# Second norm: the shift added behind the transposes, by ScalarE and VectorE, instead of ahead of them by GpSimd

## The chip, the cores and the metric

One core of a Trainium2 chip runs the kernel. Its engines run side by side, each through its own list of instructions in order: TensorE (PE; PEld is its weight load), VectorE (DVE), ScalarE (ACT), GpSimd (POOL) and SyncE (SP, which issues DMAs). Engines wait for each other by semaphores. The metric is the device time of one execution in microseconds, median of several runs.

## What is computed

A transformer block over 512 tokens of width 1024: an adaptive norm, three attention branches, gates, an output projection, a second adaptive norm and a feed-forward layer. What matters here stands behind the output projection:

```python
x = x + gate1 * (merged @ w_o[l])

u2 = rmsnorm(x, norm_mlp[l]) * (1.0 + scale2) + shift2
h = jnp.square(jax.nn.relu(u2 @ w_ff1[l]))
x = x + gate2 * (h @ w_ff2[l])
```

`shift2` has 1024 values, one for each feature; `u2` is 512 tokens by 1024 features.

## The kernel before

All products are float32 accuracy out of three products of rounded parts: each operand is split into a high part (a rounded copy, written by ACT) and a low part (the operand less its high part, written by DVE or POOL). For `u2` these are the tiles `u2h` and `u2l`.

Tokens lie in four tiles of 128 (t = 0 to 3), features in two halves of 512 (g = 0, 1). The output projection (`token_major`, tiles `po`, weights `hi_wo`, `lo_wo`) makes tokens in rows: first the left half of the features for all tokens, then the right half, each in the order tokens 0, 1, then 2, 3. Behind each right half comes the second norm of that tile of tokens, in this chain:

- `put_x1`: DVE multiplies the product by the gate (`ot`, L1208), POOL adds x (L1209), ACT takes squares and the root (L1212, L1214).
- `norm2` (L1227): DVE inverts the root and makes `tn` = x times 1/rms times (1 + scale) for each half (L1232); POOL adds the shift `b2` (L1233). `b2` is a row of 1024 values that was copied to all 128 partitions by `bcast`; in the profile it is called `bc_b`.
- `turn2` (L1235): PE turns the half's four blocks of 128x128 into one PSUM bank (`u2p`), so that features lie on the partitions.
- `split2` (L1240): ACT copies the bank into `u2h`, DVE writes the bank less `u2h` into `u2l`.

I call the work of `split2` on one (t, g) a group; there are eight, in the order (0,0), (0,1), (1,0), (1,1), (2,0), (2,1), (3,0), (3,1). The PSUM banks for `u2p` rotate among three (tag "S").

Then the feed-forward layer begins in `ff1_halves`, with the first 512 of its columns taken in two halves of tokens (0, 1, then 2, 3), four outputs of 24 products each (L1290, `pf`). The first half stands while tokens 2, 3 are still being normed. The weights' own splits (`hi_f`, `lo_f`, L224 and L236) are put between the groups on the same engines.

The order on every engine is fixed by hand: `Flow` counts the products that PE is given, and a step put with `flow.at(n, ...)` is written to its engine's list when n more have been given:

```python
flow.at(14, lambda: norm2(t))
for g in range(2):
    flow.at((30, 28, 31, 29)[t] + 6 * g, lambda g=g: turn2(t, g))
    flow.at((33, 31, 34, 32)[t] + 6 * g, lambda g=g: split2(t, g))
```

Of the kernel before, what the change touches and what calls it, by code (L numbers as in the profile page):

```python
# [13 lines left out]
F32 = mybir.dt.float32  # L14
F32R = mybir.dt.float32r
AF = mybir.ActivationFunctionType
ALU = mybir.AluOpType
# [102 lines left out]
def block_kernel(ctx: ExitStack, tc: tile.TileContext, x, c, rel_bias, ada_w, ada_b, norm_mix, w_in,  # L120
                 gate_b, diff_lambda, diff_subln, dsa_kv_norm, dsa_w_uv, w_br_a, w_br_b, w_br_c, w_o,
                 norm_mlp, w_ff1, w_ff2, norm_final, onehot, out):
    nc = tc.nc
# [16 lines left out]
    def bank(tag, name):  # L140
        return ps.tile([128, 512], F32, tag=tag, name=name, bufs=banks[tag])

    def big_tile(name, dt=F32, shape=(128, 8, 512)):
        return big.tile(list(shape), dt, tag="big", name=name)
# [284 lines left out]
    for a, b, tag in ((0, 512, "S"), (512, 640, "T")):  # L429
        tps = bank(tag, f"tps{a}")  # L430
# [274 lines left out]
    bias = {}  # L705
# [220 lines left out]
    mod = dram.tile([4, 1024], F32, name="mod")  # L926
# [253 lines left out]
    mx = mixing.enter_context(tc.tile_pool(name="mx", bufs=1))  # L1180

    def bcast(pool, name, src):
        t = pool.tile([128, 1024], F32, name=f"bc_{name}")
        nc.gpsimd.dma_start(t, bass.AP(tensor=src.tensor, offset=src.offset, ap=[[0, 128], [1, 1024]]))
        return t
# [5 lines left out]
        nc.gpsimd.dma_start(x1[:, t], x[t * 128:(t + 1) * 128])  # L1191
    a2 = bcast(mx, "a2", mod[2:3])
    nmb = bcast(mx, "nm", norm_mlp)
    b2 = bcast(mx, "b2", mod[1:2])

    def hs(h):
        return slice(h * 512, (h + 1) * 512)

    sq = {t: s1(f"sq{t}", 2) for t in range(NT)}
    tns, tps = {}, {}  # L1200
    sq_early = s1("sq_early")
    u2h, u2l = big_tile("u2h", F32R), big_tile("u2l", F32R)

    def put_x1(h):
        def evac(t, p):
            xs, ss = x1[:, t, hs(h)], sq[t]
            tt = mx.tile([128, 512], F32, tag="t5", name=f"ot{h}{t}", bufs=3)
            nc.vector.tensor_tensor(tt, p, g1[:, hs(h)], op=ALU.mult)  # L1208
            nc.gpsimd.tensor_tensor(xs, xs, tt, op=ALU.add)  # L1209

            def square():
                nc.scalar.activation(tt, xs, AF.Square, accum_out=ss[:, h:h + 1])  # L1212
                if h == 1:
                    nc.scalar.activation(ss[:, 1:2], ss[:, 1:2], AF.Sqrt, bias=ss[:, 0:1], scale=1.0 / D)  # L1214

            flow.at(9, square)
            if h == 0:
                flow.at(14, lambda: nc.vector.tensor_scalar(ss[:, 0:1], ss[:, 0:1], 1.0 / D, EPS, op0=ALU.mult,
                                                            op1=ALU.add))
            else:  # L1220
# [4 lines that stand above are left out]
        return evac  # L1225

    def norm2(t):  # L1227
        r = sq[t][:, 1:2]
        nc.vector.reciprocal(r, r)
        for g in range(2):  # L1230
            tn = tns[t, g] = mx.tile([128, 512], F32, tag="tn", name=f"tn{t}{g}", bufs=4)
            nc.vector.scalar_tensor_tensor(tn, x1[:, t, hs(g)], r, a2[:, hs(g)], op0=ALU.mult, op1=ALU.mult)  # L1232
            nc.gpsimd.tensor_tensor(tn, tn, b2[:, hs(g)], op=ALU.add)  # L1233

    def turn2(t, g):  # L1235
        tp = tps[t, g] = bank("S", f"u2p{t}{g}")
# [1 line left out]
            nc.tensor.transpose(tp[:, k * 128:(k + 1) * 128], tns[t, g][:, k * 128:(k + 1) * 128], ident)  # L1238

    def split2(t, g):  # L1240
        tv = tps[t, g].rearrange("p (k q) -> p k q", k=4)
        dh = u2h[:, 4 * g:4 * g + 4, t * 128:(t + 1) * 128]
        nc.scalar.activation(dh, tv, AF.Copy)
        nc.vector.tensor_tensor(u2l[:, 4 * g:4 * g + 4, t * 128:(t + 1) * 128], tv, dh.bitcast(F32), op=ALU.subtract)

    flow.run(token_major(["wo00", "wo01"], mh, ml, ((0, 1), (2, 3)), put_x1(0), "po0", PAIR))
    nc.vector.scalar_tensor_tensor(a2, a2, 1.0, nmb, op0=ALU.add, op1=ALU.mult)
# [334 lines left out]
```

## Time and profile before

| | us |
|---|---|
| median of three runs | 843.79 |
| the three runs | 839.05, 843.79, 844.58 |
| the profiled execution, whole | 841.24 |
| its span, first to last instruction | 839.5 |

The profiled execution's own time is 1.74 us over its span. PE is busy for 96% of the span, so a time can be won or lost only where PE waits or is made to wait; the stretch that the change touches lies between 455 us (its loads) and 520 us (the second half of the first `ff1` columns).

### The profile page before, as it was taken

Reading aid. Unit: us, or ns where it says so; the run is one execution under the profiler, and the core shown is the slowest. Engines: PE = TensorE matmul, PEld = TensorE weight load, DVE = VectorE, ACT = ScalarE, POOL = GpSimd, SP = SyncE. Lnnn points to the kernel's source line nnn. Section 1 sums busy time; section 2 is a strip of 40 time slices with the busy share of each in tenths; the row PEclk is TensorE's granted clock in tenths of the full one; section 3 lists DMA queues with packets and bytes.
Section 4 is the critical chain, followed back from the end, with each engine's and each line's share of the span. In section 5 each row is a group of like instructions: output and inputs, shape, how many; then the busy total and the mean of one; then the engine's idle time right before and its main releaser. Section 6 shows DMA issues by size and latency. Waiting matters only on the chain. (4 is left out here: it accounts for less than half of the span.)

```text
span 839.5 us, 10498 instructions
## 1 busy us (share of the span) xinstructions
PE 808.7 (96%) x3865; PEld 644.8 (77%) x3865; DVE 570.8 (68%) x992; ACT 411.7 (49%) x712; POOL 186.9 (22%) x130
## 2 busy tenths in 40 slices
PE   5899999999999999899999989999999999999996
PEld 4778867678777776557787879888888888888885
DVE  5866785678878359885445685874678567857554
ACT  7655634552434365345652446554553356335433
POOL 2014322202562224552247370000000000010020
PEclk9999999999999999999999999999999999999998
DMA  9946451133656376512135528113511441172202
GB/s 308 347 136 207 172 195 66 51 100 110 196 194 215 95 264 189 164 35 92 50 101 197 206 68 322 60 51 114 188 50 51 162 140 50 51 248 102 99 4 100
DMA packets 81535, 116.48 MB, mean 139 GB/s; under 512 B 4590, under 2 KB 53274, under 8 KB 81484
## 3 DMA queue, kind: packets, MB, share of 16 engines
q1 hardware_dynamic: 78812, 107.73, 39.0%
q0 software_dynamic: 2672, 8.09, 2.7%
q8 instruction: 30, 0.49, 0.2%
q14 instruction: 21, 0.17, 0.1%
HBM read 110.25 MB, written 8.17 MB: 141 GB/s over the span
## 5 line engine op out<-in xcount | busy, mean ns | idle before, releaser
L1266 PE MATMUL pf<-u2h,hi_f 128*128 128x512 f32 x224 | 87.1, 389 | 0.0
L1268 PE MATMUL pf<-u2l,hi_f 128*128 128x512 f32 x224 | 87.1, 389 | 0.0
L1270 PE MATMUL pf<-u2h,lo_f 128*128 128x512 f32 x224 | 87.1, 389 | 0.0
L947 DVE SCALAR_TENSOR_TENSOR adacc<-adch,cond,adacc 128x512 f32<-128x512 f32 x56 | 61.5, 1098 | 3.9 <-DMA adch<-in_ada_w_dram 3.4
L236 DVE TENSOR_TENSOR lo_f<-raw_f,hi_f 128x1024 fp32r<-128x1024 f32 x38 | 46.6, 1255 | 16.9 <-ACT hi_f L224 16.9
L1436 POOL DMA_DIRECT2D x1f<-x1d x4 | 2.1, 537 | 234.3 <-PE pp L1412 234.3
L224 ACT ACTIVATE hi_p<-w 128x1024 fp32r<-128x1024 f32 x36 | 36.3, 1050 | 34.0 <-PE pp L1412 27.1
L236 DVE TENSOR_TENSOR lo_p<-w,hi_p 128x1024 fp32r<-128x1024 f32 x36 | 42.7, 1221 | 9.8 <-ACT hi_p L224 9.8
L224 ACT ACTIVATE hi_f<-raw_f 128x1024 fp32r<-128x1024 f32 x38 | 38.6, 1048 | 21.5 <-PE p2l L1528 7.1
L1270 PEld LDWEIGHTS pf<-u2h,lo_f 128*128 128x128 f32 x224 | 42.0, 188 | 8.7
L1266 PEld LDWEIGHTS pf<-u2h,hi_f 128*128 128x128 f32 x224 | 42.0, 188 | 8.7
L1268 PEld LDWEIGHTS pf<-u2l,hi_f 128*128 128x128 f32 x224 | 42.0, 188 | 8.7
L1412 PE MATMUL pp<-hi_p,hq 128*128 128x512 f32 x144 | 45.8, 389 | 0.0
L236 POOL TENSOR_TENSOR lo_gb<-raw_gb,hi_gb 128x1024 fp32r<-128x1024 f32 x8 | 20.0, 2519 | 65.3 <-ACT hi_gb L224 65.3
L1412 PEld LDWEIGHTS pp<-hi_p,hq 128*128 128x128 f32 x144 | 27.0, 188 | 5.6
L726 ACT ACTIVATE Pa<-Pa,nma 128x128 f32<-128x128 f32 (+3 forms) x32 | 17.7, 554 | 27.7 <-DVE nma L722 27.6
L1412 PE MATMUL pp<-hi_p,he 128*128 128x512 f32 x96 | 30.5, 389 | 0.0
L1412 PE MATMUL pp<-hi_p,ha 128*128 128x512 f32 x96 | 30.5, 389 | 0.0
L1406 DVE TENSOR_TENSOR acc<-acc,pp 128x512 f32<-128x512 f32 x32 | 21.7, 683 | 10.6 <-PE pp L1412 10.6
L236 POOL TENSOR_TENSOR lo_gc<-raw_gc,hi_gc 128x1024 fp32r<-128x1024 f32 x8 | 19.2, 2413 | 41.7 <-ACT hi_gc L224 41.7
L1412 PE MATMUL pp<-lo_p,hq 128*128 128x512 f32 x72 | 28.1, 390 | 0.0
L527 PE MATMUL p_gb<-uh,hi_gb 128*128 128x512 f32 x64 | 27.5, 430 | 0.0
(429 smaller groups left out, 2329.2 us busy)
## 6 DMA issues: line engine op xcount, KB each, us to landing
raw_f<-in_w_ff_dram SPq DMA_DIRECT2D x20, 1024.0 KB
adch<-in_ada_w_dram SPq DMA_DIRECT2D x64, 256.0 KB
w<-in_w_ff_dram SPq DMA_DIRECT2D x12, 1024.0 KB
ada<-in_ada_w_dram SPq DMA_DIRECT2D x32, 256.0 KB
raw_gc<-in_w_in_dram SPq DMA_DIRECT2D x4, 1024.0 KB
raw_gb<-in_w_in_dram SPq DMA_DIRECT2D x4, 1024.0 KB
raw_a<-in_w_in_dram SPq DMA_DIRECT2D x4, 1024.0 KB
raw_ga<-in_w_in_dram SPq DMA_DIRECT2D x4, 1024.0 KB
```

Of the source, the lines that this page charges most:

```text
L224: nc.scalar.activation(parts[n][0][:, sl], raws[n][:, sl], AF.Copy)
L236: eng.tensor_tensor(parts[n][1][:, sl], raws[n][:, sl], parts[n][0][:, sl].bitcast(F32), op=ALU.subtract)
L527: nc.tensor.matmul(dst, wh[:, k, cs], uh[:, k], start=k == 0, stop=False)
L726: nc.scalar.activation(p[:, 0:w], p[:, 0:w], AF.Exp, bias=nm, scale=-1.0, accum_out=sm)
L947: nc.vector.scalar_tensor_tensor(acc, ach[n], cond[:, k:k + 1], acc, op0=ALU.mult, op1=ALU.add)
L1266: nc.tensor.matmul(dst, wh[:, i, cs], u2h[:, i], start=i == 0, stop=False)
L1268: nc.tensor.matmul(dst, wh[:, i, cs], u2l[:, i], start=False, stop=False)
L1270: nc.tensor.matmul(dst, wl[:, i, cs], u2h[:, i], start=False, stop=i == KT - 1)
L1406: nc.vector.tensor_tensor(c, c, dst[t], op=op)
L1412: nc.tensor.matmul(dst[t], a[:, part, k, j, ts_], w[:, k], start=not onto and k == 0 and m == 0, stop=k == 3 and m == 2, skip_group_check= ...
L1436: nc.gpsimd.dma_start(x1f[:, t], x1d[t * 128:(t + 1) * 128])
```

## The change

The shift is no longer copied to all partitions. It is loaded as a tile of 128 partitions by 8, one feature a partition and one column for each block of 128 features. POOL's eight adds go. In `split2` the four blocks of a bank are now taken one by one: ACT writes the high part of the block plus its column of the shift, and DVE writes the block plus the column less the high part in one instruction.

```diff
     a2 = bcast(mx, "a2", mod[2:3])
     nmb = bcast(mx, "nm", norm_mlp)
-    b2 = bcast(mx, "b2", mod[1:2])
+    b2 = mx.tile([128, 8], F32, name="b2")
+    nc.gpsimd.dma_start(b2, mod[1:2].rearrange("o (k p) -> p (o k)", p=128))
...
             nc.vector.scalar_tensor_tensor(tn, x1[:, t, hs(g)], r, a2[:, hs(g)], op0=ALU.mult, op1=ALU.mult)
-            nc.gpsimd.tensor_tensor(tn, tn, b2[:, hs(g)], op=ALU.add)
...
     def split2(t, g):
-        tv = tps[t, g].rearrange("p (k q) -> p k q", k=4)
-        dh = u2h[:, 4 * g:4 * g + 4, t * 128:(t + 1) * 128]
-        nc.scalar.activation(dh, tv, AF.Copy)
-        nc.vector.tensor_tensor(u2l[:, 4 * g:4 * g + 4, t * 128:(t + 1) * 128], tv, dh.bitcast(F32), op=ALU.subtract)
+        for k in range(4):
+            tv, b = tps[t, g][:, k * 128:(k + 1) * 128], b2[:, 4 * g + k:4 * g + k + 1]
+            dh, dl_ = (u[:, 4 * g + k, t * 128:(t + 1) * 128] for u in (u2h, u2l))
+            nc.scalar.activation(dh, tv, AF.Identity, bias=b)
+            nc.vector.scalar_tensor_tensor(dl_, tv, b, dh.bitcast(F32), op0=ALU.add, op1=ALU.subtract)
```

Below, "waits X" names the semaphores of the engines (or DMA queues) that an instruction waits for. This is what stood on ACT before, from the squares of tokens 1 to the last group of tokens 0, 1:

```order
L1212 ACTIVATE ot_4229,sq_4015<-x_4000 128x512 [waits Pool_49]
L1214 ACTIVATE sq_4015<-sq_4015 128x1 [waits Activation_49]
L1243 ACTIVATE u2h<-u2p_4268 128x4x128 [waits PE_49]
L224 ACTIVATE hi_f_4289<-raw_f_4193 128x1024 [waits DMAHW7_49,PE_49]
L1243 ACTIVATE u2h<-u2p_4281 128x4x128 [waits PE_49]
L224 ACTIVATE hi_f_4289<-raw_f_4193 128x1024
L1243 ACTIVATE u2h<-u2p_4295 128x4x128 [waits PE_49]
L1243 ACTIVATE u2h<-u2p_4310 128x4x128 [waits PE_49]
```

Each group was one activation, which waited for PE alone. The same place on ACT now:

```order
L1215 ACTIVATE sq_4015<-sq_4015 128x1 [waits Activation_49]
L1244 ACTIVATE u2h<-u2p_4264,b_4012 128x128 [waits DMASW3_49,PE_49]
L1244 ACTIVATE u2h<-u2p_4264,b_4012 128x128 [waits DVE_49] x3
L224 ACTIVATE hi_f_4291<-raw_f_4193 128x1024 [waits DMAHW7_49,PE_49]
L1244 ACTIVATE u2h<-u2p_4283,b_4012 128x128 [waits PE_49]
L1244 ACTIVATE u2h<-u2p_4283,b_4012 128x128 [waits DVE_49] x3
L224 ACTIVATE hi_f_4291<-raw_f_4193 128x1024
L1244 ACTIVATE u2h<-u2p_4303,b_4012 128x128 [waits PE_49]
L1244 ACTIVATE u2h<-u2p_4303,b_4012 128x128 [waits DVE_49] x3
```

A group is now four activations, of which the first waits for PE and the other three for DVE. On DVE the groups of tokens 0, 1 stood so, behind the last `tn`:

```order
L1232 SCALAR_TENSOR_TENSOR tn_4261<-x_4000,sq_4015,bc_a_4008 128x512 [waits Pool_49]
L1244 TENSOR_TENSOR u2l<-u2p_4268,u2h 128x4x128 [waits Activation_49]
L1244 TENSOR_TENSOR u2l<-u2p_4281,u2h 128x4x128 [waits Activation_49]
L1244 TENSOR_TENSOR u2l<-u2p_4295,u2h 128x4x128 [waits Activation_49]
L236 TENSOR_TENSOR lo_f_4290<-raw_f_4193,hi_f_4289 128x1024 [waits DMAHW7_49]
L1208 TENSOR_TENSOR ot_4317<-po_4232,bc_g_4002 128x512 [waits PE_49]
L1244 TENSOR_TENSOR u2l<-u2p_4310,u2h 128x4x128 [waits Activation_49]
```

Now, on DVE, at the same place:

```order
L1233 SCALAR_TENSOR_TENSOR tn_4258<-x_4000,sq_4015,bc_a_4008 128x512 [waits Pool_49]
L1245 SCALAR_TENSOR_TENSOR u2l<-u2p_4264,b_4012,u2h 128x128 [waits DMASW3_49,Activation_49]
L1245 SCALAR_TENSOR_TENSOR u2l<-u2p_4264,b_4012,u2h 128x128 [waits Activation_49] x3
L1245 SCALAR_TENSOR_TENSOR u2l<-u2p_4283,b_4012,u2h 128x128 [waits Activation_49] x4
L1245 SCALAR_TENSOR_TENSOR u2l<-u2p_4303,b_4012,u2h 128x128 [waits Activation_49] x4
L236 TENSOR_TENSOR lo_f_4292<-raw_f_4193,hi_f_4291 128x1024 [waits DMAHW7_49]
L1209 TENSOR_TENSOR ot_4331<-po_4232,bc_g_4002 128x512 [waits PE_49]
L1245 SCALAR_TENSOR_TENSOR u2l<-u2p_4324,b_4012,u2h 128x128 [waits Activation_49] x4
```

The places in the lists are the same; each low part became four, and each of the four waits for an activation. (The lines of the changed kernel are one higher from L1195 on.)

## Rows read from the trace of the kernel before

**Rows 1.** The page: busy time, share of the span and instructions of each engine.

```profile
PE 808.7 (96%) x3865; PEld 644.8 (77%) x3865; DVE 570.8 (68%) x992; ACT 411.7 (49%) x712; POOL 186.9 (22%) x130
```

**Rows 2.** Waits from 480 to 515 us: us in total, times, longest.

```profile
PE u2p L1238 <- POOL tn L1233: 2.4, 2, 1.6
```

**Rows 3.** PE's timeline: start, us, instruction, idle time before and releaser.

```profile
485.75 0.66 PE L1238 MATMUL u2p<-ident,tn 128*128 128x128 f32 x4 [1.65 <-POOL tn L1233]
...
494.69 0.28 PE L1290 MATMUL pf<-u2h,hl_f 128*128 128x256 f32 x1
...
503.94 0.66 PE L1238 MATMUL u2p<-ident,tn 128*128 128x128 f32 x4 [0.74 <-POOL tn L1233]
...
509.41 0.28 PE L1290 MATMUL pf<-u2h,hl_f 128*128 128x256 f32 x1
509.53 0.28 PE L1290 MATMUL pf<-u2l,hl_f 128*128 128x256 f32 x1
```

**Rows 4.** DVE's timeline, 484 to 515 us.

```profile
484.68 3.27 DVE L1232 SCALAR_TENSOR_TENSOR tn<-x,sq,bc_a 128x512 f32<-128x512 f32 x2
...
489.42 0.69 DVE L1244 TENSOR_TENSOR u2l<-u2p,u2h 128x512 fp32r<-128x512 f32 x1 [0.86 <-ACT u2h L1243]
...
491.46 1.22 DVE L236 TENSOR_TENSOR lo_f<-raw_f,hi_f 128x1024 fp32r<-128x1024 f32 x1
492.59 0.69 DVE L1208 TENSOR_TENSOR ot<-po,bc_g 128x512 f32<-128x512 f32 x1
...
496.01 2.15 DVE L1232 SCALAR_TENSOR_TENSOR tn<-x,sq,bc_a 128x512 f32<-128x512 f32 x2
...
514.25 0.43 DVE L1371 TENSOR_TENSOR e<-e 128x256 f32<-128x256 f32 x1 [3.81 <-ACT e L1370]
```

**Rows 5.** ACT's timeline, 486 to 515 us.

```profile
486.44 0.60 ACT L1243 ACTIVATE u2h<-u2p 128x512 fp32r<-128x512 f32 x1 [2.00 <-PE u2p L1238]
487.84 1.06 ACT L224 ACTIVATE hi_f<-raw_f 128x1024 fp32r<-128x1024 f32 x1 [0.80 <-PE po L834]
488.81 0.58 ACT L1243 ACTIVATE u2h<-u2p 128x512 fp32r<-128x512 f32 x1
...
514.71 0.63 ACT L1360 ACTIVATE he<-e 128x512 fp32r<-128x512 f32 x1 [0.55 <-DVE e L1371]
```

**Rows 6.** POOL's timeline, 455 to 490 us.

```profile
455.24 0.54 POOL L1184 DMA_DIRECT2D bc_b<-mod  x1
457.90 1.28 POOL L1209 TENSOR_TENSOR x<-x,ot 128x512 f32<-128x512 f32 x1 [2.12 <-DMA x<-in_x_dram]
...
483.99 6.37 POOL L1233 TENSOR_TENSOR tn<-tn,bc_b 128x512 f32<-128x512 f32 x4 [0.63 <-DVE tn L1232]
```

**Rows 7.** Groups by line and form: busy us, mean ns of one, idle before.

```profile
L609 ACT ACTIVATE kjunk<-tpk 128x128 f32<-128x128 f32 x4 | 1.1, 278 | 0.7 <-PE tpk L604 0.6
...
L787 ACT ACTIVATE zb<-p_gb,vcol 128x512 f32<-128x512 f32 x8 | 5.5, 685 | 13.9 <-PE p_gb L531 13.9
...
L726 ACT ACTIVATE Pa<-Pa,nma 128x128 f32<-128x128 f32 x8 | 3.2, 395 | 5.4 <-DVE nma L722 5.4
...
L1083 DVE SCALAR_TENSOR_TENSOR Pa<-Pa,sma,Pa 128x128 f32<-128x128 f32 x4 | 1.4, 352 | 0.1
...
L722 DVE CUSTOM_DVE_ANT_0 Pa<-sa,T 128x128 f32<-128x128 f32 x8 | 2.0, 285 | 1.4 <-PE sa L1067 1.4
```

**Rows 8.** The tile `tn`: durations in ns (least, median, most), first and last start.

```profile
L1232 DVE SCALAR_TENSOR_TENSOR tn<-x,sq,bc_a x8: 736/1524/1784, 482.2 to 502.0; 128x512 f32<-128x512 f32 x8
```

**Rows 9.** Windows: busy us of PE, PEld, DVE, ACT, POOL; granted clock; DMA.

```profile
116.00:118.00 2.00, 0.15 (x3) 0.11 (x2) 1.82 (x4) 0.72 (x3) 1.69 (x1) 1.00 0.26 105
...
119.00:122.00 3.00, 3.00 (x9) 1.55 (x9) 2.02 (x8) 0.32 (x3) 0.00 (x0) 0.55 1.03 362
```

**Rows 10.** DMA: a queue's packets, MB and share of 16 engines; an issue's us to landing.

```profile
q0 software_dynamic: 2672, 8.09, 2.7%
...
bc_b<-mod POOLq DMA_DIRECT2D x1, 512.0 KB, 13.7
```

## The prediction

> **What bounds the kernel now.** I began with the page: PE is busy for 96% of the span [rows 1], so the question is where PE waits in the stretch that the change touches. The list of waits for that stretch has PE wait for POOL's add of the shift twice, 2.4 us in all [rows 2]; PE's timeline shows where: 1.65 us ahead of the first transposes at 485.75, and 0.74 us ahead of those at 503.94 [rows 3]. This is all that the removal of POOL's adds can give PE directly. Then I read the engines that work beside PE there. POOL's four adds for tokens 0, 1 fill 6.37 us and start at 483.99, when DVE's first `tn` is done [rows 6]; the pair of `tn` on DVE that runs beside them takes 3.27 us, though the fastest single one takes 0.736 us [rows 4, 8]. ACT and DVE hand over at once: the high part of 488.81 ends at 489.39 and its low part starts at 489.42, and in the other direction `e` ends at 514.68 and `he` starts at 514.71, so 0.03 us each way [rows 4, 5]. A group takes 0.58 + 0.03 + 0.69 = 1.3 us today.
>
> **What goes.** POOL's eight adds leave the chain. PE could start the first transposes at 485.75 - 1.65 = 484.10, and the wait of 0.74 goes: 2.4 us, if nothing new is late. DVE's `tn` pair of token tile 1 loses POOL's company and takes 2 x 0.736 = 1.47 us for 3.27 [rows 4, 8].
>
> **What is added.** A group is now four high parts and four low parts. In the order of the changed kernel the second to fourth activation of a group wait for DVE, and in the built program the value waited for rises by one from each to the next, to the low part just ahead. So ACT and DVE take turns: high, low, high, low. Nothing of a group overlaps, and behind the waiting activation stand ACT's next splits of weights, behind the waiting low part DVE's.
>
> The rows of before can't show whether the turns are needed, for there the low part needs the whole high part anyway (489.39 to 489.42). The Trainium skill, page "PSUM — Partial Sum Buffer", section "PSUM bank collisions raise a hardware error", says that two engines must not use one bank and quadrant of PSUM at the same time, reads included, and that the compiler's back end orders them; the four blocks of a group lie in one bank. By that rule the turns stay and the sum below holds; if ACT could run ahead, the chain would stay hidden and the sum would be the first rival's.
>
> The price of one turn: the high part of 128x128 out of PSUM takes 0.278 us without a bias (L609); a bias from a tile makes 0.685 out of 0.60 at 512 columns [rows 5, 7], 0.085 more: 0.363. Its lower bound is 0.278, its upper 0.395, a 128x128 activation with a bias (L726). The low part is a scalar_tensor_tensor of 128x128; from SBUF it takes 0.352 (L1083), which I take. Below it lies another DVE operation that reads PSUM, 0.285 (L722), above it a tensor_tensor of twice the columns, 0.43 [rows 4, 7]. With 0.06 for the two handovers one turn takes 0.363 + 0.352 + 0.06 = 0.775 us, between 0.623 and 0.885. A group goes from 1.3 us to about 3.
>
> **The new chain, step by step.** Tokens 0, 1. PE transposes from 484.10, ACT's first high part follows 0.69 later as now (485.75 to 486.44) [rows 3, 5], but DVE is busy with `tn` until 484.68 + 1.47 = 486.15. Low parts of group 1 start there, the last 3 x 0.775 later, and ACT's last high part ends at 488.44. Then `hi_f`, 0.97 from start to start (487.84 to 488.81) [rows 5]: group 2 starts at 489.4 and ACT's share of it takes 3 x 0.775 + 0.363 = 2.69, to 492.1. `hi_f` again, group 3 from 493.06 to 495.75 on ACT, and its last low part ends at 496.13. On DVE `lo_f` (1.13 from start to start) and `ot` (some 0.6) come next [rows 4], so group 4's low parts start at 497.86 and end at 497.86 + 3 x 0.775 + 0.352 = 500.54; ACT's last high part ends at 500.15. The first feed-forward product started at 494.69 and its output took 24 x 0.12 = 2.88 us, to 497.57 [rows 3]. Now PE reaches it 1.65 us earlier, finds the operands missing, follows the turns, and gets the last at 500.54; two more products, 500.78. PE is 3.2 us late, the 1.65 us it had won being gone with the rest.
>
> Tokens 2, 3. From `ot` to `tn` it was 496.01 - 492.59 = 3.42 us, of which 0.69 is `ot` and 1.28 POOL's add of x [rows 4, 6]; the square, the root and the reciprocal are the other 1.45. ACT can begin them only when group 4 is off, at 500.15: `tn` at 501.6, 2.15 as now to 503.75 (POOL still adds the x of tile 3 beside it), `lo_f` to 504.9, and the last `tn` pair, 1.47 and a little for its reciprocal, to 506.5. Groups 5 to 8 follow without a break; the next group's first high part runs beside the last low part, so a group costs 3 x 0.775 + 0.352 + 0.03 = 2.71. The last low part ends at 506.5 + 3 x 2.71 + 2.68 = 517.3. PE by itself would reach the second half at about 500.78 + 72 x 0.12 + 4 x 0.66 for the transposes = 512.1 [rows 3], well ahead, so the chain decides: the first output of the second half, which ended at 509.41 + 2.88 = 512.29 [rows 3], now ends at 517.3 + 0.24 = 517.55.
>
> **The sum** is +5.3 us. Behind it PE, busy for 96% of the span [rows 1], has little that could take it up, and I take the loads and stores that hang on DVE's `lo_f` of this stretch to move back by about as much, not more. Against its own time the profiled execution goes from 841.24 to 846.5. About 24 turns lie on the chain, and eight single parts: the lower prices take off 24 x 0.152 + 0.6 = 4.2, the upper add 24 x 0.11 + 0.5 = 3.1. So +1.1 to +8.4. The median of the runs lies 2.55 over the profiled one, and the mean of all four is 842.2; I put the sum on this mean: 847.4.
>
> The load of the shift is put at nothing: one issue replaces one of 0.54 us, and POOL waits 2.12 us behind it [rows 6], which hides a longer one up to that. 512 KB less are written.
>
> **The rivals.**
> The turns don't cost: if ACT were free to run ahead, or a turn took under some 0.5 us, each group would end about when it does now and PE would keep the 2.4 us: 838.8. For it speaks only that PE's first need comes late; against it the waits in the program. 0.08.
>
> The load is late, and the kernel ends slower. The shift becomes 1024 pieces of 4 bytes. It is issued at 455.24 and needed at 484.8, so it decides from 29.5 us to landing on; the old one landed after 13.7 [rows 10]. A packet of this queue takes 0.027 x 16 x 839.5 / 2672 = 0.136 us [rows 10]; 1024 of them on 16 engines are 8.7 us, which is hidden; all on one engine would be 139 us, landing at 594, and every us past 484.8 would be paid in full: some 950. The Trainium skill, "DMA: Bandwidth & Descriptors", "Rules for kernel authors", says that a strided last dimension becomes one descriptor for each element; no run here shows such a transfer. 0.05.
>
> The clock: PE's longest new pause is between group 3's last low part and group 4's first, 496.4 to 498.2. After 2 us with 0.15 us of work the granted clock was 0.55 over 3 us, mostly the lower of its levels, 1.2 instead of 2.4 GHz [rows 9]; the pause of 1.65 us today had no such sequel. That costs 3 x 0.45 = 1.4 us of PE, hidden while the chain leads, paid if it falls behind 517: 848.8. 0.07.
>
> **How the numbers follow.** The forecast has 0.80. 1% is 8.4 us, about what a measurement of this kernel can tell from no change, and the forecast's upper end touches it: I give 0.06 to slower there, 0.05 to the late load, 0.04 to the clock on top of dear turns: 0.15. Faster by over 1% would need more than PE waits here: 0.01. The range goes from 841.24 + 1.1 to 842.2 + 8.4 rounded up for the clock: 842 to 851.
>
> **What would show it.** POOL has no adds behind the x of tokens; the transposes at 485.75 come at about 484; the activations of L1244 wait for DVE, 24 times, and the low parts for ACT; eight groups of about 3 us; PE's waits move from `u2p` to `pf` at L1291, for ACT and DVE, 3 us and more in each half; the last low part at about 517 on the old time axis. Groups of 1.5 us or a `pf` without waits would refute it; a wait for the DMA at the first L1244 would mean the second rival.

## The result, and the profile after

The changed kernel takes 847.45 us (median of 10 runs, 844.43 to 849.93); the kernel before, beside it on the same chip, 841.78 us (10 runs, 839.05 to 844.58). The ratio is 1.0073 [1.0059, 1.0087]: slower by 6.1 us, between 5.0 and 7.3, and so by less than 1% (8.4 us). The prediction had 847.4.

The profiled execution after took 847.76 us, its span is 845.4. In it POOL's add of x for token tile 1, the last step ahead of the stretch that the change touches, starts at 483.41 us; before it started at 482.07. To compare times of after with those of the prediction, take off 1.34 us; I write these as "on the old axis".

The page's busy line of after, to be held against [rows 1], and its section on the DMA queue that POOL issues to:

```profile
PE 814.4 (96%) x3865; PEld 648.2 (77%) x3865; DVE 572.5 (68%) x1016; ACT 417.8 (49%) x736; POOL 174.3 (21%) x122
...
q0 software_dynamic: 2560, 7.57, 2.6%
```

POOL has its eight instructions fewer, ACT and DVE 24 more each. PE does the same 3865 products, and yet is called busy for 5.7 us more: products that crawl behind missing operands, or run at a lower clock, count as busy (a pair of feed-forward products that follows the turns is listed with 0.56 us, where 0.40 is usual). So the page alone doesn't show the loss; the list of waits shows where to look. Of after, 480 to 522 us (us in total, times, longest):

```profile
ACT u2h L1244 <- DVE u2l L1245: 14.8, 24, 2.5
DVE u2l L1245 <- ACT u2h L1244: 12.2, 26, 0.9
PEld pf L1291 <- DVE u2l L1245: 3.2, 9, 1.6
PE pf L1291 <- DVE u2l L1245: 1.4, 1, 1.4
PE u2p L1238 <- DVE u2l L1245: 0.6, 1, 0.6
```

POOL is gone from PE's waits [rows 2]. In its place PE and its weight loads wait for DVE's low parts, and ACT and DVE wait for each other: ACT 24 times, three for each of the eight groups. That is the turn, seen closest in the timelines of after, first ACT's, then DVE's, at group 1:

```profile
486.02 0.37 ACT L1244 ACTIVATE u2h<-u2p,b 128x128 fp32r<-128x128 f32 x1 [0.22 <-PE u2p L1238]
487.74 0.37 ACT L1244 ACTIVATE u2h<-u2p,b 128x128 fp32r<-128x128 f32 x1 [1.35 <-DVE u2l L1245]
488.52 0.37 ACT L1244 ACTIVATE u2h<-u2p,b 128x128 fp32r<-128x128 f32 x1 [0.42 <-DVE u2l L1245]
489.31 0.37 ACT L1244 ACTIVATE u2h<-u2p,b 128x128 fp32r<-128x128 f32 x1 [0.42 <-DVE u2l L1245]
```

```profile
486.02 1.41 DVE L1233 SCALAR_TENSOR_TENSOR tn<-x,sq,bc_a 128x512 f32<-128x512 f32 x2
487.36 0.34 DVE L1245 SCALAR_TENSOR_TENSOR u2l<-u2p,b,u2h 128x128 fp32r<-128x128 f32 x1
488.14 0.35 DVE L1245 SCALAR_TENSOR_TENSOR u2l<-u2p,b,u2h 128x128 fp32r<-128x128 f32 x1 [0.44 <-ACT u2h L1244]
488.92 0.35 DVE L1245 SCALAR_TENSOR_TENSOR u2l<-u2p,b,u2h 128x128 fp32r<-128x128 f32 x1 [0.43 <-ACT u2h L1244]
...
501.20 0.35 DVE L1245 SCALAR_TENSOR_TENSOR u2l<-u2p,b,u2h 128x128 fp32r<-128x128 f32 x1 [0.44 <-ACT u2h L1244]
...
505.97 1.42 DVE L1233 SCALAR_TENSOR_TENSOR tn<-x,sq,bc_a 128x512 f32<-128x512 f32 x2
...
509.65 0.61 DVE L1245 SCALAR_TENSOR_TENSOR u2l<-u2p,b,u2h 128x128 fp32r<-128x128 f32 x2 [0.44 <-ACT u2h L1244]
...
517.52 0.35 DVE L1245 SCALAR_TENSOR_TENSOR u2l<-u2p,b,u2h 128x128 fp32r<-128x128 f32 x1 [0.44 <-ACT u2h L1244]
```

Read them against each other: DVE 487.36, ACT 487.74, DVE 488.14, ACT 488.52, DVE 488.92. One turn is 0.785 us, and each engine is idle for more than half of it. The pair of `tn` takes 1.41 us for 3.27 [rows 4]. PE's timeline of after at the places that answer to [rows 3], the first transposes, the first feed-forward product, the worst pause, and the first product of the second half:

```profile
485.35 0.63 PE L1238 MATMUL u2p<-ident,tn 128*128 128x128 f32 x4
...
494.50 0.38 PE L1291 MATMUL pf<-u2h,hl_f 128*128 128x256 f32 x1 [0.32 <-ACT u2h L1244]
...
499.24 0.53 PE L1291 MATMUL pf<-u2l,hl_f 128*128 128x256 f32 x1 [1.36 <-DVE u2l L1245]
...
513.67 0.28 PE L1291 MATMUL pf<-u2h,hl_f 128*128 128x256 f32 x1
```

The first transposes stand at 484.01 on the old axis and wait no more (485.75 before); PE reaches the feed-forward product at 493.16 (494.69 before), 1.53 us early. Then it loses all of that and more: the second half begins at 512.33 on the old axis, 2.92 us late (509.41 before).

### The profile page after: what moved, and what is told of

Its sections match the earlier page's. It is cut to its first block, busy times and chain, and to the rows that moved or that the text cites. A ratio compares the mean times of both kernels' runs of the same rounds, so it can differ in the third digit from the quotient of the medians.

```text
span 845.4 us, 10529 instructions
## 1 busy us (share of the span) xinstructions
PE 814.4 (96%) x3865; PEld 648.2 (77%) x3865; DVE 572.5 (68%) x1016; ACT 417.8 (49%) x736; POOL 174.3 (21%) x122
```

## The experiments

Differences in us are worked out from the ratios unless the text says otherwise. Each kernel was timed beside the kernel before. The first four shared a chip and one set of runs of before (841.79 us, 29 runs), the other three another (842.19 us, 29 runs). In the diffs, lines with - are of the kernel named. To follow a difference inside the traces I also give, on the old axis, where PE starts the third output of the second half (its rows change there from `hl_f` to `hi_f`, and all groups are done by then); before, that is at 515.17.

**1. The same instructions without the turns.** From the changed kernel; all four activations of a group are written first, then its four low parts.

```diff
-        for k in range(4):
-            tv, b = ...
-            dh, dl_ = ...
+        ks = [(tps[t, g][:, k * 128:(k + 1) * 128], b2[:, 4 * g + k:4 * g + k + 1],
+               u2h[:, 4 * g + k, ...], u2l[:, 4 * g + k, ...]) for k in range(4)]
+        for tv, b, dh, _ in ks:
             nc.scalar.activation(dh, tv, AF.Identity, bias=b)
+        for tv, b, dh, dl_ in ks:
             nc.vector.scalar_tensor_tensor(dl_, tv, b, dh.bitcast(F32), op0=ALU.add, op1=ALU.subtract)
```

> The changed kernel, but a group's four activations are written first and its four low parts behind them; the same instructions, no turns. If the turns are the cause, ACT's part of a group takes some 1.2 us and DVE's some 1.15 us, different groups overlap, the feed-forward products hardly wait, and the time is 1 to 3 us under before. If the cause is that four small instructions cost more than one large one, it stays 4 to 6 us over before.

Measured: 840.2 us (12 runs), ratio 0.9982 [0.9966, 0.9999]. It is 1.5 us under the kernel before, if by a narrow margin, where the changed kernel is 6.1 over, so it beats both. Its timeline, ACT's first high parts and DVE's low parts:

```profile
484.00 1.14 ACT L1244 ACTIVATE u2h<-u2p,b 128x128 fp32r<-128x128 f32 x4 [0.22 <-PE u2p L1238]
```

```profile
485.34 1.12 DVE L1246 SCALAR_TENSOR_TENSOR u2l<-u2p,b,u2h 128x128 fp32r<-128x128 f32 x4
487.50 1.13 DVE L1246 SCALAR_TENSOR_TENSOR u2l<-u2p,b,u2h 128x128 fp32r<-128x128 f32 x4 [1.04 <-ACT u2h L1244]
```

Four activations end to end take 1.14 us and four low parts 1.12, against 4 x 0.785 in turns: single ones overlap in part with the next on their own engine, and there is one handover instead of seven. The single instructions are as long as in the changed kernel. From the groups by form, of after and then of this kernel (least, median, most in ns):

```profile
L1244 ACT ACTIVATE u2h<-u2p,b x32: 358/368/371, 486.0 to 517.1; 128x128 fp32r<-128x128 f32 x32
```

```profile
L1244 ACT ACTIVATE u2h<-u2p,b x32: 348/370/437, 484.0 to 503.1; 128x128 fp32r<-128x128 f32 x32
```

So what cost the time is the alternation, not smaller or more instructions, nor the bias. In the list of waits of this kernel for the same stretch, PE has none on ACT, DVE or POOL; ACT and DVE wait for each other 4 times instead of 50:

```profile
DVE u2l L1246 <- ACT u2h L1244: 2.9, 4, 1.0
ACT u2h L1244 <- PE u2p L1238: 2.7, 5, 0.8
```

**2. The load alone.** The kernel before with one more load, the 128x8 gather of the shift, whose tile nobody reads.

```diff
+    b2c = mx.tile([128, 8], F32, name="b2c")
+    nc.gpsimd.dma_start(b2c, mod[1:2].rearrange("o (k p) -> p (o k)", p=128))
```

> The kernel before with the load of the shift as 128 by 8 added behind the others, unused. If the load in 1024 pieces costs the core anything by itself (POOL's issue, the DMA engines), the time rises by some of the 5 to 6 us; if the turns are the cause, it stays within 1 us of before.

Measured: 841.76 us (12 runs), ratio 0.9998 [0.9984, 1.0012]. The load costs nothing that can be seen. In the changed kernel the issue on POOL and the landing (the last number, us from issue) answer to [rows 6, 10]:

```profile
456.61 0.94 POOL L1195 DMA_DIRECT2D b<-mod  x1
```

```profile
b<-mod POOLq DMA_DIRECT2D x1, 4.0 KB, 13.1
```

The issue takes 0.94 us where that of the 512 KB took 0.54; POOL waits behind it, and the tile is there some 16 us before its first use at 486.02.

**3. The adds alone.** The kernel before without POOL's eight adds; the shift is left out of the result.

```diff
-            nc.gpsimd.tensor_tensor(tn, tn, b2[:, hs(g)], op=ALU.add)
```

> The kernel before without POOL's eight adds: the shift of the second norm is left out of the result. It gives what the removal of the adds is worth by itself. From the two waits of PE: 2.4 us under before, by every theory; if something next in line is as late as POOL was, 0 to 1 us under.

Measured: 838.74 us (12 runs), ratio 0.997 [0.9958, 0.9982], so 2.5 us less, between 1.5 and 3.5. This is all that the removal of the adds can give, and it is the size of PE's two waits for POOL [rows 2]. In the profiled execution the gain is larger: the third output of the second half starts at 511.70, 3.5 us early. The batch of experiment 1 reaches 1.5 us by its ratio, and the intervals overlap; its trace has the third output at 511.65, so up to there the batch loses nothing of the gain.

**4. The turns alone.** The kernel before with POOL's adds kept and no bias: plain copies and subtractions, in four turns for a group.

```diff
-        tv = tps[t, g].rearrange("p (k q) -> p k q", k=4)
-        dh = u2h[:, 4 * g:4 * g + 4, t * 128:(t + 1) * 128]
-        nc.scalar.activation(dh, tv, AF.Copy)
-        nc.vector.tensor_tensor(u2l[:, 4 * g:4 * g + 4, ...], tv, dh.bitcast(F32), op=ALU.subtract)
+        for k in range(4):
+            tv = tps[t, g][:, k * 128:(k + 1) * 128]
+            dh, dl_ = (u[:, 4 * g + k, t * 128:(t + 1) * 128] for u in (u2h, u2l))
+            nc.scalar.activation(dh, tv, AF.Copy)
+            nc.vector.tensor_tensor(dl_, tv, dh.bitcast(F32), op=ALU.subtract)
```

> The kernel before, POOL's adds kept, but each group in four turns of a plain activation and a plain subtraction. If the turns are the cause, it is 3 to 6 us over before (a turn without bias some 0.64 us, 24 of them on the chain, and the first group starts 1.7 us later than in the changed kernel). If the bias, the fused low part or the load is the cause, it stays within 1 us of before.

Measured: 845.54 us (6 runs), ratio 1.0055 [1.0038, 1.0073]: 4.6 us more, with no shift moved at all. Its list of waits and two low parts of its timeline:

```profile
ACT u2h L1244 <- DVE u2l L1245: 13.8, 24, 2.6
PE u2p L1238 <- POOL tn L1233: 3.8, 2, 2.1
PE pf L1291 <- DVE u2l L1245: 1.3, 1, 1.3
```

```profile
490.16 0.29 DVE L1245 TENSOR_TENSOR u2l<-u2p,u2h 128x128 fp32r<-128x128 f32 x1 [0.34 <-ACT u2h L1244]
490.79 0.29 DVE L1245 TENSOR_TENSOR u2l<-u2p,u2h 128x128 fp32r<-128x128 f32 x1 [0.34 <-ACT u2h L1244]
```

A turn without the bias is 0.63 us, and the same 24 waits are there. The late turns also push the second `tn` and POOL's adds behind it: PE's waits for POOL grow from 2.4 to 3.8 us, and after the longer of them, 2.13 us, the granted clock is 0.74, 0.50, 0.50 and 0.55 in the four microseconds from 506 on, 1.7 us of PE at full speed. PE then does the first 48 products of the second half without a break, in 5.76 us, so what counts here is how late PE comes, not the last groups. So the turns bring a loss even where no shift is moved, though part of it comes here by way of POOL and the clock; the move of the shift is the gain.

**5. Two pieces at a time.** From the changed kernel: two activations, their two low parts, then the other two (`ks` as in experiment 1; the loop it replaces is left out).

```diff
+        n = 2
+        for k0 in range(0, 4, n):
+            for tv, b, dh, _ in ks[k0:k0 + n]:
+                nc.scalar.activation(dh, tv, AF.Identity, bias=b)
+            for tv, b, dh, dl_ in ks[k0:k0 + n]:
+                nc.vector.scalar_tensor_tensor(dl_, tv, b, dh.bitcast(F32), op0=ALU.add, op1=ALU.subtract)
```

> The changed kernel, with the group of four pieces written two at a time: two activations, their two low parts, then the other two. Same instructions; one wait back (ACT for DVE's low part) per group where the changed kernel has three. Theory of the turns: a group loses one wait back and takes about 2.6 us instead of about 3.1, in chains about 2.3 us per group instead of 3.1, so the time lies between: 0 to 3 us over the kernel before, where the changed kernel is 5.7 over and the batch of four 1.6 under. Rival, that any wait back inside a group costs the whole: 5 us or more over.

Measured: 841.4 us (12 runs), ratio 0.9994 [0.9981, 1.0008]: 0.5 us under before, between 1.6 under and 0.7 over: just under the 0 to 3 over that the theory gave, with an interval that reaches into it, and far from the rival's 5 us. DVE's timeline:

```profile
484.78 0.60 DVE L1248 SCALAR_TENSOR_TENSOR u2l<-u2p,b,u2h 128x128 fp32r<-128x128 f32 x2
486.08 0.61 DVE L1248 SCALAR_TENSOR_TENSOR u2l<-u2p,b,u2h 128x128 fp32r<-128x128 f32 x2 [0.69 <-ACT u2h L1246]
```

Half a group is 1.30 us, the group about the expected 2.6. The cost rises with the number of returns, but not in proportion: against before, three for each group give +6.1 us, one -0.5, none -1.5.

**6 and 7. Where the turns stand.** From the changed kernel: turns in the groups of tokens 0, 1 only, then in those of tokens 2, 3 only, with the loops of experiment 5 and

```diff
-        n = 2      (experiment 5)
+        n = 1 if t < 2 else 4      (6)
+        n = 1 if t > 1 else 4      (7)
```

> The changed kernel with turns in the groups of token tiles 0 and 1 only; the groups of tiles 2 and 3 have four activations and then four low parts. The prediction's list of steps: first feed-forward output 3.2 us late, the last pair of tn near 506.5 as in the changed kernel, then groups 5 to 8 are closer and end near 511, so that TensorE itself sets the second half (about 512): 2 to 3.5 us over the kernel before. Rival, that a turn costs the same wherever it stands: half of the 7.3 us between the changed kernel and the batch of four, so about 2 us over; this run alone does not tell the two apart, the run with turns last does.

> The changed kernel with turns in the groups of token tiles 2 and 3 only; the groups of tiles 0 and 1 have four activations and then four low parts. The prediction's list of steps: nothing late in the first half, the last pair of tn near 499, groups 5 to 8 in turns end near 510, about when TensorE comes to need them: within 1 us of the batch of four, so 1 to 2.5 us under the kernel before. Rival, that a turn costs the same wherever it stands: half of the 7.3 us, about 2 us over the kernel before.

Measured: turns first, 844.55 us, ratio 1.0038 [1.0023, 1.0052], 3.2 us over before by the ratio; turns last, 840.63 us, ratio 0.9989 [0.9972, 1.0005], 0.9 us under (12 runs each), a little short of the 1 to 2.5 under that were expected. The rival gave both about 2 us over, which the interval of turns last excludes (its upper end is 0.4 us). A turn's price depends on its place, as the prediction's steps have it. The final pair of `tn` and the low parts behind it, from DVE's timelines, turns first and then turns last:

```profile
504.17 1.41 DVE L1233 SCALAR_TENSOR_TENSOR tn<-x,sq,bc_a 128x512 f32<-128x512 f32 x2
505.50 3.18 DVE L1248 SCALAR_TENSOR_TENSOR u2l<-u2p,b,u2h 128x128 fp32r<-128x128 f32 x12
509.31 1.13 DVE L1248 SCALAR_TENSOR_TENSOR u2l<-u2p,b,u2h 128x128 fp32r<-128x128 f32 x4 [0.63 <-ACT u2h L1246]
```

```profile
497.81 1.42 DVE L1233 SCALAR_TENSOR_TENSOR tn<-x,sq,bc_a 128x512 f32<-128x512 f32 x2
...
509.36 0.35 DVE L1248 SCALAR_TENSOR_TENSOR u2l<-u2p,b,u2h 128x128 fp32r<-128x128 f32 x1 [0.44 <-ACT u2h L1246]
```

With turns first the final `tn` starts at 504.60 on the old axis (add 0.43), as in the changed kernel (504.63); PE, late from the first half, comes to the second half at 511.47 (511.04 in its own trace), when all low parts are there, and does the 48 products of its first two outputs in 5.76 us, without a break. With turns last the final `tn` starts at 498.48 (add 0.67), 6.1 us earlier, and PE comes to the second half at 506.17, much as in the batch (505.89), but its first 48 products take 7.47 us, 1.7 more, strung out between the turns. In the changed kernel they take 7.46 (513.67 to 521.13). So the changed kernel has both losses: the first groups' turns make everything behind late, the last groups' turns cost PE 1.7 us. By the ratios, against the batch, turns first cost 4.7 us, turns last 0.6 and both 7.7; the intervals, about 1.3 us either way for each, don't tell whether the two simply add up. In the traces they nearly do: against the batch, the third output of the second half is 5.6 us late with turns first (517.23), 2.0 with turns last (513.64) and 8.1 with both (519.79).

## Why the prediction was right

**The gain, 2.4 us:** experiment 3 has 2.5 by its ratio, but 3.5 at the third output of its trace, so the term was rather too small. The list counts a wait from the listed end of the product ahead (0.39 us for a product of 512 columns, though the next one starts after 0.23). By the starts of its products, PE of before loses 1.8 us ahead of 485.75, 0.9 ahead of 503.94, and 0.15 and 0.3 ahead of the transposes at 489.16 and 501.59: some 3.2 us. It doesn't enter the sum, where the new chain decides.

**The price of a turn, 0.775 us:** measured 0.785. The activation with a bias from a tile takes 0.368 (0.363 was put together from the cost of a bias at 512 columns and a bare activation), the low part 0.350 (0.352), and the two handovers 0.067 (0.06). The low part was priced by a row that read SBUF only; here it reads PSUM and is no slower.

**That ACT can't run ahead:** all 24 waits are there. Within one PSUM bank the two engines alternate; between banks they don't, for the row at 509.65 has the last low part of one group and the first of the next back to back, so ACT had written the next high part meanwhile. Even in the batch of experiment 1 a low part starts just when the group's last activation ends. This agrees with the rule of the page "PSUM — Partial Sum Buffer", section "PSUM bank collisions raise a hardware error", of the Trainium skill. The order is put in by waits in the program, though; whether the chip could do without wasn't tried. And since each bank is one tile here, the runs can't tell whether the waits go by the bank or by the tile.

**The chain, step by step** (predicted, and measured on the old axis):

| | predicted | measured |
|---|---|---|
| low parts of group 1 start | 486.15 | 486.02 |
| last low part of group 4 ends | 500.54 | 500.21 |
| first `tn` of tokens 2, 3 starts | 501.6 | 500.99 |
| last `tn` pair ends | 506.5 | 506.05 |
| PE at the second half | 512.1 | 512.33 |
| one of the last groups | 2.71 | 2.62 |
| last low part ends | 517.3 | 516.53 |

The small miss that builds up is in the groups: a low part and the next group's first one overlap in part (0.61 for two), where I had added the full 0.352 + 0.03. That PE comes to the second half so near the forecast is in part luck: I had put 4 x 0.66 us on the transposes there, and by their starts they take some 1.5; the rest is made up by a wait for DVE, the 0.60 us at the last transposes that the list names, and by the lower clock below.

**The sum, +5.3 us:** the third output of the second half, which comes when all of this is done, starts at 521.13, on the old axis 519.79, against 515.17 before: +4.6. PE's rows, of before and then of after:

```profile
515.17 0.28 PE L1290 MATMUL pf<-u2h,hi_f 128*128 128x256 f32 x1
```

```profile
521.13 0.28 PE L1291 MATMUL pf<-u2h,hi_f 128*128 128x256 f32 x1
```

The two spans, 845.4 and 839.5, differ by 5.9, of which 1.34 was there ahead of the stretch: 4.6 again, so nothing is taken up or added behind it. The medians differ by 5.7. About half of the 1 us between lies outside the span: a whole execution takes 2.31 us more than its span in the mean of the 10 runs of after, and 1.79 in that of 29 runs of before; why isn't shown. The other half is put to no step; runs of one kernel spread over 5 us. That the forecast of 847.4 meets the median to 0.1 us is luck, then: it stood on a mean of 842.2, which more runs put at 841.78, and the sum was short of the medians by as much. Because of this spread experiment 1, whose profiled execution was 2.2 us under its median, is 3.5 us ahead at this point and only 1.5 in the medians.

**The load at nothing:** experiment 2. Its 1024 pieces don't appear as packets. In experiment 2, which adds the load and takes nothing away, the queue has 32 more than the 2672 of before [rows 10]:

```profile
q0 software_dynamic: 2704, 8.10, 2.8%
```

So the second rival, which counted a packet for each piece, had its price wrong. What the traces count is packets, so they neither bear out nor refute the Trainium skill, page "DMA: Bandwidth & Descriptors", section "Rules for kernel authors", on one descriptor for each element; they show that the whole was there after 13.1 us.

**What I had wrong** is how PE would show it. I expected waits of 3 us and more in each half; the list has 1.7 us for PE on `pf` in the first half, and in the second only the 0.6 on `u2p`. The rest is in products strung out between the turns (some of it listed for the weight loads, 3.2 us in all), and in the clock that the third rival named. Windows of 1 us of after (busy PE, PEld, DVE, ACT, POOL; then the granted clock):

```profile
498.00:499.00 1.00, 0.00 (x0) 0.00 (x0) 1.00 (x3) 0.00 (x0) 0.00 (x0) 1.00 0.00 0
499.00:500.00 1.00, 0.76 (x3) 0.69 (x3) 0.54 (x2) 0.37 (x1) 1.00 (x1) 0.66 0.00 0
500.00:501.00 1.00, 1.00 (x5) 0.90 (x5) 0.35 (x1) 0.58 (x2) 0.28 (x1) 0.50 0.00 0
501.00:502.00 1.00, 1.00 (x6) 0.93 (x6) 0.80 (x2) 0.97 (x4) 0.00 (x0) 0.50 0.00 0
502.00:503.00 1.00, 1.00 (x7) 1.00 (x7) 0.96 (x3) 0.10 (x1) 0.77 (x1) 0.63 0.00 0
```

After the pause ahead of 499.24 the clock is at its lower level, 1.2 GHz, or partly so for 4 us: 0.34 + 0.50 + 0.50 + 0.37 = 1.7 us of PE at full speed, at most. It was hidden, as that rival said it would be while the chain leads: PE came to the second half at 512.33 on the old axis, and its operands were complete at 516.53. Experiment 6 has the same pause (1.37 us) and the same fall. Experiment 4 has a pause in the same place, nearly as long, without a fall, and falls only after its second, longer one:

```profile
499.75 0.39 PE L1291 MATMUL pf<-u2l,hl_f 128*128 128x256 f32 x1 [1.32 <-DVE u2l L1245]
505.95 0.66 PE L1238 MATMUL u2p<-ident,tn 128*128 128x128 f32 x4 [2.13 <-POOL tn L1233]
```

No run has the turns of the changed kernel without the fall, so that it cost nothing there is read from the rows and not tested.

## What to carry to other kernels

When one engine's work is folded into instructions of two others that read the same PSUM bank, write all of the first engine's instructions for that bank and then all of the second's; a loop that writes both for each piece makes them take turns, and turned a gain of 1.5 us into a loss of 6. Before pricing smaller instructions by their durations, look in the built program at what each waits for: the durations here were as expected, and the waits between them decided. And the same twelve turns cost some 4 us more where the next tokens' norm was queued behind them than where nothing was.

## What was not expected of the hardware

The granted clock fell after a pause of 1.36 us, while before, after one of 1.65 us at 484.10 [rows 3], it had not: before, PE was busy for all of the 2 us from 482 to 484, ahead of the pause; after, for 1.68 us from 494 to 496 and 1.87 us from 496 to 498, while it followed the turns. In experiment 4, where the clock held through a pause of 1.32 us, PE was busy for all of 494 to 498, and it still fell after the next pause, of 2.13 us. What decides isn't shown. And a load of 4 KB, one value to each of 1024 places, landed 13.1 us after its issue, hardly earlier than 512 KB in whole rows (13.7), and its issue kept POOL longer, 0.94 us against 0.54.
